# Full attention with every engine's order written out, small jobs in a queue, and row sums through a column of ones

## The chip, the cores and the metric

The kernel runs on one core of one Trainium2 chip. The metric is the device time of one execution in microseconds (us). Engine names are those of the profile: PE (TensorE matmuls), PEld (its weight loads), DVE (VectorE), ACT (ScalarE), POOL (GpSimd), SP (SyncE, which issues most DMAs).

## The reference

Input x has 1024 tokens (a grid of 16 rows by 64 columns) of width 1024. Cut to what matters:

```
h = rmsnorm(x)                                  # gain_in
p = h @ w                                       # 1024 x 3328: q,k,v of A; q,k,v of B; gates of A and of B
A: 8 query heads, 2 key/value heads, D = 64; q, k RMS-normalised per head, 2-D axial rotary positions;
   softmax(q k^T / 8) v over all 1024 keys
B: 8 heads, D = 64; each token sees 8 grid rows x 16 columns around it;
   softmax(q k^T / 8 + relative bias, masked) v
y = concat(A * silu(gate_a), B * silu(gate_b)) @ w_out
out = rmsnorm(x + y)                            # gain_out
```

Everything is float32 in and out.

## The kernel before

Weights come in 17 groups of 256 columns, g = 0 to 12 of w and 13 to 16 of w_out. A product in near float32 accuracy is three fp16 matmuls: the activations and the weights are each split into hi (fp16 of the scaled value) and lo (fp16 of the rest), and hi·hi, hi·lo and lo·hi go to one PSUM tile. So a weight group is loaded by POOL's queue (L158), squared by ACT for its scale (L280), summed over partitions by a tiny matmul (L292) whose result DVE and POOL turn into the scale (L293, L294), split into hi by ACT (L299, two halves) and lo by DVE (L306, two halves); PE then uses it (L368). Two raw tiles rotate: group g + 2 is loaded once g is split.

Four stages follow one another. The **head** loads and normalises x, transposes it and projects the groups that A needs. **A** has 64 units, each a head and a block of 128 queries. A unit does QK into a PSUM tile of 128x1024 (L591, L593), the row maximum on DVE (L600, called MAX below), the exponential on ACT in fp32 (L602) with the row sum in its accumulator, its fp16 hi on ACT (L603), its lo on DVE (L608, LO), one DMA transpose of hi and lo on SP (L613) and, four units later, 24 matmuls with V's hi and lo (L622 to L624, pv). After every fourth unit DVE divides by the row sums (L628 to L631). **B** has 64 units, each a head and a block of 128 queries with two or three key blocks (256 or 384 keys): QK (L674, L675), biased maximum on DVE (L682, L684), two exponentials on ACT (L685 with its accumulator, L686), LO on DVE (L691), transpose, pv five units later (L704 to L706), division and gate (L711 to L716). The biases are built ahead by DVE from a loaded table and a mask (L648), one instruction of 128x1536 for each of four tables. The **tail** has the output rows that are left: row u of eight needs its mixture squared, scaled and split (L732 to L744, called os(u)), transposed (L749), and 24 matmuls for each of four groups, added to the residual (L773) and normalised (L797 to L807).

One object, `Flow`, keeps the order. Each unit is a slot (`step`): "pre" callbacks, QK and MAX, "mid" callbacks, LO of the unit before, "post" callbacks, then `fill(n)`, which takes n pieces of six projection matmuls from a queue, then pv of an older unit. `at(delay, pos, fn)` puts a callback into a later slot. FILL_A and FILL_B give n by slot. PE's order is always that of the code; in A and B, before, the order of ACT, DVE, POOL and SP is the scheduler's, which may put a ready instruction ahead of an earlier one. SPLIT_AT says after which unit of B os(u) starts.

Of the kernel before, what the change touches and what calls it, by code (L numbers as in the profile page):

```python
# [8 lines left out]
F32 = mybir.dt.float32  # L9
# [13 lines left out]
NX = 4  # L23
SKEW_A, SKEW_B = 4, 5
# [5 lines left out]
PREP = {2: 4, 3: 0, 4: 2, 12: 0, 13: 0}  # L30
# [3 lines left out]
AREA = 34816  # L34
RING = 5
SLOTS = {"both": (16384, 2048, 4), "qc": (24576, 2048, 2), "stg1": (28672, 2048, 3), "stg": (18432, 2048, 3),
         "t": (0, 1536, 5), "ptb": (7680, 1536, 5), "ob": (15360, 1024, 1), "th": (16384, 16384, 2), "y": (16384, 2048, 1),
         "p32": (AREA + 14336, 1536, 2)}
BIAS = {(0, 0): ("ar", 18432), (0, 1): ("rq", 8192), (1, 0): 0, (1, 1): 1}
# [4 lines left out]
class Flow:  # L44


    def __init__(self):
        self.slot = 0
        self.due = {}
        self.queue = []  # L50
        self.credit = 0.0

    def at(self, delay, pos, fn, *a):
        self.due.setdefault((self.slot + delay, pos), []).append((fn, a))

# [18 lines left out]
    def step(self, n, first=None, second=None, last=None):  # L74
        self.run("pre")
        if first:
            first()
        self.run("mid")
        if second:
            second()  # L80
        self.run("post")
        self.fill(n)
        if last:
            last()
        self.run("end")
        self.slot += 1
# [3 lines left out]
def kernel(ctx: ExitStack, tc: tile.TileContext, x: bass.AP, w: bass.AP, wo: bass.AP,  # L90
# [14 lines left out]
    at = fl.at  # L105
# [8 lines left out]
    ar = one.tile([P, 25, 512], F32, name="ar").rearrange("p a b -> p (a b)")  # L114
# [39 lines left out]
    def load_w(g):  # L154
# [3 lines left out]
        pool.dma_start(raw[g], w[g] if g < 13 else wo[g - 13])  # L158

# [73 lines left out]
    def x_sq(u, e):  # L233
        xhl[u] = one.tile([P, 2, 1024], F16, tag=f"m{u % 4}", name=f"xhl{u}")
# [35 lines left out]
    def prep_a(g):  # L270
# [7 lines left out]
        wss[g] = tn(f"wss{g}", 1, "ws")  # L278
        if g:
            act.activation(wp[g][0].bitcast(BF16), raw[g], AF.Square, accum_out=wss[g])  # L280
            return
        late["half"] = tn("wssh", 1, "ws")
        act.activation(wp[g][0][:, :4].bitcast(BF16), raw[g][:, :4], AF.Square, accum_out=late["half"])

    def prep_a2(g):
        dve.tensor_tensor_reduce(out=wp[g][0][:, 4:].bitcast(BF16), in0=raw[g][:, 4:], in1=raw[g][:, 4:], scale=1.0,
                                 scalar=late["half"], op0=OP.mult, op1=OP.add, accum_out=wss[g])

    def prep_b(g):
        pt = ahead.append(proj_tile(f"wt{g}")) or ahead[-1]  # L290
        top = [a.bitcast(BF16)[:, 1:2] for a in (mh[:, :1], wss[g])]
        pe.matmul(pt[:, 0, :1], top[0].to_broadcast([P, P]), top[1], start=True, stop=True)  # L292
        dve.tensor_scalar(wss[g], pt[:, 0, :1], -2.0 ** -27, 1e-30, op0=OP.mult, op1=OP.add)  # L293
        pool.tensor_tensor(col(S_ + g), wss[g], mh[:, :1], op=OP.pow)  # L294
# [6 lines left out]
    def prep_d(g):  # L301
# [7 lines left out]
        if g > 14:  # L309
            t = wraw.tile([P, 2, 1024], F32, tag="raw", name=f"x2{g}")  # L310
            for i in range(2):
                x2[2 * g - 26 + i] = t[:, i]
                load_x2(2 * g - 26 + i)

    ready = set()
# [18 lines left out]

    def prep(g):
        d = PREP.get(g, 1)
        at(d + 1, "pre", prep_a, g)
        at(d + 2, "mid", pend.append, g)

    def sums_now():  # L340

        while pend:
            g = pend.pop(0)
            prep_b(g)
            at(1, "pre", prep_c, g)
            at(1, "post", prep_d, g)
            if g + 2 < 17:
# [27 lines left out]
    def proj_pair(g, up, lhs, evac):  # L375

        pt = proj_tile(f"pj{g}_{up}")
        assert g in ready
# [15 lines left out]
    va = r6(1, [P, NU, 2, 2, D], F16, "va")  # L394
# [57 lines left out]
    def kva_gen(up):  # L452
        def evac(pt):
# [3 lines left out]
            at(1, "pre", lambda: act.activation(va[:, 2 * up:2 * up + 2, :, 0, :], vs, AF.Copy, scale=2.0 ** -14))  # L457

            def vlo():
                for i in range(2):  # L460
                    dve.scalar_tensor_tensor(va[:, 2 * up + i, :, 1, :], vs[:, i], 2.0 ** -14,
                                             va[:, 2 * up + i, :, 0, :], op0=OP.mult, op1=OP.subtract)
# [26 lines left out]
    def qb_gen(hh, up):  # L489
        def evac(pt):  # L490
# [15 lines left out]
            at(1, "pre", hi)  # L506
            at(1, "mid", lo)
# [536 lines left out]
```

## Time and profile before

| what | value |
|---|---|
| median of 3 runs | 604.59 us (600.97 to 606.09) |
| the profiled execution's own time | 600.28 us |
| its span | 598.5 us |
| mean granted TensorE clock | 0.974 |
| busy in the span: PE, DVE, ACT, POOL | 530.8, 440.9, 391.0, 121.8 us |
| stages on the span: head, A, B, tail | 0 to 105, to 352, to 557, to 598.5 us |

A window row of the profile reads: its bounds, its length, then for PE, PEld, DVE, ACT and POOL the busy time and the count of instructions in brackets, then the granted clock (1.00 is full), the mean busy share of the 16 DMA engines and GB/s. A wait row reads: engine, operation and line that waited, what released it, then total us, times and the longest. A group row reads: line, engine, operation, out<-in, shapes, count, then busy us and mean ns of one, then idle time ahead of it and its releasers. A timeline row reads: start, duration, engine, line, operation, and in brackets idle time ahead of it.

### The profile page before, as it was taken

The numbers are of one execution on the slowest core, as the hardware profiler recorded it, in microseconds if no ns is written. First come the engines' busy times: TensorE is split into PE (matmuls) and PEld (weight loads), VectorE is DVE, ScalarE is ACT, GpSimd is POOL, SyncE is SP. The second block draws the span as 40 slices with busy tenths as digits, with TensorE's granted clock in tenths as the row PEclk, the third lists the DMA queues.
The fourth block names the chain that finished last, engine by engine and source line by source line (L and its number), as shares of the span: only waits on it lengthen the run. The fifth ranks groups of instructions, "written<-read, shape, count | busy, mean of one in ns | idle before, by whom it ended". The sixth has DMA issues, their size and how long they took to land.

```text
span 598.5 us, 13870 instructions
## 1 busy us (share of the span) xinstructions
PE 530.8 (89%) x5541; PEld 404.4 (68%) x5541; DVE 440.9 (74%) x986; ACT 391.0 (65%) x647; POOL 121.8 (20%) x150
## 2 busy tenths in 40 slices
PE   2587989979979989998989979999999789889894
PEld 1366878758856545556768857887877567668684
DVE  4689676987978968975988947585878767778332
ACT  5553445777768858875868826677779986774210
POOL 2395788510100000000100000010111221122100
PEclk9979989989999989999899999999999899999898
DMA  8989533799999999999899983467576996699422
GB/s 233 225 162 243 112 108 68 143 187 215 195 192 188 206 209 181 221 191 208 179 188 213 230 214 79 90 133 96 128 116 123 180 200 146 138 146 190 92 61 70
DMA packets 245972, 97.26 MB, mean 162 GB/s; under 512 B 236562, under 2 KB 237202, under 8 KB 243987
## 3 DMA queue, kind: packets, MB, share of 16 engines
q1 hardware_dynamic: 242306, 75.66, 70.8%
q0 software_dynamic: 3312, 19.92, 11.7%
q8 instruction: 43, 0.70, 0.5%
q10 hardware_dynamic: 288, 0.79, 0.5%
q14 instruction: 23, 0.18, 0.1%
HBM read 31.33 MB, written 4.19 MB: 59 GB/s over the span
## 4 chain that ended last, share of the span: by engine, by line
PE 48%; DMA 18%; DVE 14%; issue 8%; ACT 5%; POOL 4%; SPq 1%; DVEq 0%; POOLq 0%; ACTq 0%
PE pj L368 15%; DMA ar<-ar 10%; PE wt L368 8%; PE kb L368 5%; PE po L368 4%; PE s L591 3%; PE s L593 3%; PE pv L622 2%; PE pv L624 2%; PE pv L623 2%; DVE whl L306 2%; DMA ar<-mhl 2%; POOL nt L416 1%; PE sb L675 1%; DMA x2b<-in_x_dram 1%
## 5 line engine op out<-in xcount | busy, mean ns | idle before, releaser
L368 PEld LDWEIGHTS <-hT 128*128 128x128 f16 x2112 | 205.8, 100 | 68.9 <-DMA hT<-xhl 14.7
L368 PE MATMUL pj<-whl,hT 128*128 128x256 f16 x1584 | 187.6, 274 | 3.9 <-DMA hT<-xhl 2.5
L602 ACT ACTIVATE ar<-s,nm,sm 128x1024 f32<-128x1024 f32 x64 | 76.9, 1202 | 43.6 <-DVE nm L600 35.8
L600 DVE CUSTOM_DVE_ANT_0 ar<-s,sm 128x1024 bf16<-128x1024 f32 x64 | 81.9, 1279 | 18.9 <-PE s L593 18.6
L368 PE MATMUL wt<-whl,hT 128*128 128x256 f16 x528 | 70.9, 294 | 13.8 <-ACT whl L299 7.1
L608 DVE TENSOR_TENSOR ar<-ar 128x1024 f16<-128x1024 f32 x64 | 77.9, 1218 | 5.4 <-ACT ar L603 5.4
L603 ACT ACTIVATE ar<-ar 128x1024 f16<-128x1024 f32 x64 | 67.5, 1056 | 6.5 <-DVE ar L608 5.3
L368 PE MATMUL po<-whl,mA 128*128 128x256 f16 x384 | 65.8, 277 | 0.0
L685 ACT ACTIVATE rq<-ar,mx,sm 128x384 f32<-128x384 f32 (+1 forms) x64 | 43.0, 672 | 30.8 <-DVE mx L684 30.6
L294 POOL TENSOR_TENSOR sm<-wss,mh 128x1 f32<-128x1 f32 x17 | 12.7, 749 | 240.4 <-DVE wss L293 160.6
L368 PEld LDWEIGHTS <-mA 128*128 128x128 f16 x512 | 48.8, 100 | 12.5 <-issue 5.3
L368 PE MATMUL po<-whl,ar 128*128 128x256 f16 x192 | 53.1, 277 | 0.0
L622 PE MATMUL pv<-va,ar 128*128 128x64 f16 x384 | 39.9, 195 | 12.0 <-DMA ar<-ar 12.0
L306 DVE SCALAR_TENSOR_TENSOR whl<-raw,sm,whl 128x1024 f16<-128x1024 f32 (+1 forms) x33 | 44.7, 1371 | 2.3 <-ACT whl L299 2.3
L622 PEld LDWEIGHTS <-ar 128*128 128x128 f16 x384 | 35.1, 99 | 16.6 <-DMA ar<-ar 14.3
L686 ACT ACTIVATE ar<-ar,mx,sm 128x384 f16<-128x384 f32 (+1 forms) x64 | 42.8, 673 | 1.0
L299 ACT ACTIVATE whl<-raw,sm 128x1024 f16<-128x1024 f32 x34 | 37.0, 1136 | 5.9 <-POOL sm L294 5.8
L624 PE MATMUL pv<-va,ar 128*128 128x64 f16 x384 | 39.9, 195 | 0.0
L623 PE MATMUL pv<-va,ar 128*128 128x64 f16 x384 | 39.8, 195 | 0.0
L591 PE MATMUL s<-kTa,rq 128*128 128x512 f16 x128 | 39.4, 391 | 0.3 <-ACT ar L602 0.3
L682 DVE CUSTOM_DVE_ANT_0 ar<-sb,bias 128x384 f32<-128x384 f32 x48 | 26.6, 554 | 17.2 <-PE sb L675 14.3
L691 DVE TENSOR_TENSOR ar<-rq,ar 128x384 f16<-128x384 f32 (+1 forms) x64 | 34.1, 533 | 4.4 <-ACT ar L686 4.4
(183 smaller groups left out, 1012.2 us busy)
## 6 DMA issues: line engine op xcount, KB each, us to landing
raw<-in_w_dram POOLq DMA_DIRECT2D x11, 1024.0 KB, 6.3
raw<-in_wo_dram POOLq DMA_DIRECT2D x4, 1024.0 KB, 6.1
ar<-in_x_dram SPq DMA_DIRECT2D x7, 512.0 KB, 6.4
khh<-ar SPq DMA_DIRECT2D x16, 128.0 KB, 4.1
x2b<-in_x_dram POOLq DMA_DIRECT2D x4, 512.0 KB, 6.4
x<-in_x_dram POOLq DMA_DIRECT2D x4, 512.0 KB, 6.3
out_dram<-x2b SPq DMA_DIRECT2D x8, 256.0 KB, 3.3
ar<-ar SPq DMA_TRANSPOSE x112, 4.5
```

Of the source, the lines that this page charges most:

```text
L306: dve.scalar_tensor_tensor(wp[g][1][:, s], raw[g][:, s], col(S_ + g), wp[g][0][:, s], op0=OP.mult, op1=OP.subtract)
L368: pe.matmul(*o[0], **o[1])
L591: pe.matmul(s[:, c * 512:(c + 1) * 512], q, kTa[:, 4 * c:4 * c + 4, hh], start=True, stop=False)
L600: dve.tensor_tensor_reduce(out=hl[:, 1].bitcast(BF16), in0=s, in1=col(SHA).to_broadcast([P, 1024]), scale=col(NSA), scalar=3e38, op0=OP.ad ...
L602: act.activation(p32, s, AF.Exp, bias=nm, scale=col(SCA), accum_out=sums[hh, u][:, h:h + 1])
L603: at(0, "post", lambda: act.activation(hl[:, 0], p32, AF.Copy))
L608: dve.tensor_tensor(hl[:, 1], p32, hl[:, 0], op=OP.subtract)
L622: pe.matmul(o, pt[:, kt], va[:, kt, hh, 0], start=kt == 0, stop=False)
L623: pe.matmul(o, pt[:, kt], va[:, kt, hh, 1], start=False, stop=False)
L624: pe.matmul(o, pt[:, 8 + kt], va[:, kt, hh, 0], start=False, stop=kt == 7)
L685: act.activation(p32, t, AF.Exp, bias=mx, scale=col(SCB + hh), accum_out=sums["b", u][:, h:h + 1])
L686: act.activation(hl[:, 0], t, AF.Exp, bias=mx, scale=col(SCB + hh))
```

## The change

Every line number of the changed kernel is about 110 to 115 higher in A and B (MAX is L713, EXP L715, HI L716, LO L721, pv L735 to L737, hi and lo of the weights L386 and L391, bias L761, B's MAX L796).

- **A by hand.** From the sixth slot of A to its end ACT, DVE, POOL and SP also follow the order of the code. In B the scheduler orders them as before.
- **Jobs with a budget.** Small work of ACT and DVE goes into a list (`job`) with a cost in us and a lateness. In each slot `work(eng)` takes the jobs due, urgent ones always, others while half their cost fits into what a slot's budget leaves (BASE_A or BASE_B plus 0.654 us per piece of filler, less the engine's fixed work). `need` forces the jobs of a weight group or an output row out before PE's first use.
- **Weights.** From group 5 squares are taken in four quarters into spare space as soon as the load is there, their sums by four tiny matmuls, hi and lo in quarters; the next load follows one slot after the last lo.
- **Column of ones.** V has 65 columns, the last one 1.0, so pv with hi of V also yields the row sum; the exponentials no longer write an accumulator, and the division reads PSUM.
- **Gates of A** do two steps on POOL and one on DVE, instead of two on DVE. **os(u)** squares one half on ACT and the other on DVE, and its steps are jobs.
- **Biases** are built by one job per head; the masks of the three tables made in B go into a tile that A's last transposed p used ("gain"), and gain_out is loaded into it at slot 16 of B.
- **Order of output work.** Rows 4, 5 and 6 are in B's queue (before, row 4 only), with other FILL_B and SPLIT_AT.

```diff
-FILL_B = [(12, 3.4), (24, 3), (2, 2.5)]
-FILL_B_END = 3
-SPLIT_AT = (26, 27, 29, 31, 39, 55, 56)
+FILL_B = [(13, 3.25), (12, 2.95), (22, 3.45)]
+FILL_B_END = 3.2
+SPLIT_AT = (22, 24, 27, 31, 39, 47, 55)
...
+    def work(self, eng):
+
+        b = self.budget.get(eng)
+        self.left[eng] = 1e9 if b is None else min(self.left.get(eng, 0.0), 0.5 * b) + b
+        while True:
+            due = sorted(j for j in self.jobs if j[3] == eng and j[1] <= self.slot and (j[0] == 0 or j[4] / 2 < self.left[eng]))
+            if not due:
+                return
+            j = due[0]
+            self.jobs.remove(j)
+            self.left[eng] -= j[4]
+            j[5](*j[6])
...
+        if self.base:
+            us = self.base[0] + 0.654 * n
+            self.budget = {"act": us - self.base[1], "dve": us - self.base[2]}
         self.run("pre")
+        self.work("act")
         if first:
             first()
-        self.run("mid")
         if second:
             second()
+        self.run("mid")
+        self.work("dve")
         self.run("post")
...
+        def lo(i):
+            q = QUARTERS[i]
+            dve.scalar_tensor_tensor(wp[g][1][:, q], raw[g][:, q], col(S_ + g), wp[g][0][:, q], op0=OP.mult, op1=OP.subtract)
+            if i < 3:
+                return
+            ready.add(g)
+            prep_e(g)
+            if g + 2 < 17:
+                at(1, "pre", load_w, g + 2)
...
-        act.activation(p32, s, AF.Exp, bias=nm, scale=col(SCA), accum_out=sums[hh, u][:, h:h + 1])
-        at(0, "post", lambda: act.activation(hl[:, 0], p32, AF.Copy))
+        act.activation(p32, s, AF.Exp, bias=nm, scale=col(SCA))
+        at(0, "mid", lambda: act.activation(hl[:, 0], p32, AF.Copy))
...
-            pe.matmul(o, pt[:, kt], va[:, kt, hh, 0], start=kt == 0, stop=False)
-            pe.matmul(o, pt[:, kt], va[:, kt, hh, 1], start=False, stop=False)
-            pe.matmul(o, pt[:, 8 + kt], va[:, kt, hh, 0], start=False, stop=kt == 7)
+            pe.matmul(o, pt[:, kt], va[:, kt, hh, v_hi], start=kt == 0, stop=False)
+            pe.matmul(o[:, :D], pt[:, kt], va[:, kt, hh, v_lo], start=False, stop=False)
+            pe.matmul(o, pt[:, 8 + kt], va[:, kt, hh, v_hi], start=False, stop=kt == 7)
...
-    run_units(ua, SKEW_A, a_qk, a_lo, a_pv, rates(FILL_A + [(64 - n_head, mid)], FILL_A_END))
-    fl.fill(1000)
-
-    gout = one.tile([P, 1024], F32, tag="gain", name="gain_o")
-    sp.dma_start(gout, dap(gain_out, 0, [[0, P], [1, 1024]]))
+    fl.base = BASE_A
+    with run_units(ua, SKEW_A, a_qk, a_lo, a_pv, rates(FILL_A + [(64 - n_head, mid)], FILL_A_END), by_hand=HAND):
+        fl.fill(1000)
+
...
+    ms = one.tile([P, 1024], F32, tag="gain", name="masks")
...
+                make = load_bias(ty, hh, ms[:, ty * 384:ty * 384 + 384], k < 2)
+                for h in range(4):
+                    job("dve", 0.5, make, h, delay=2 + 2 * k, late=1)
```

The first place is DVE in the second row block of A, where a weight group is split into lo. In the names nm is a unit's row maximum, s its scores, ar its exponentials, whl the split weights, raw the loaded ones. Before:

```order
L600 ISA ar,nm_6_1_2429<-s_6_1_2424,sm 128x1024
L600 ISA nm_6_1_2429 128x1
L318 RECIPROCAL sm<-sm 128x1
L608 TENSOR_TENSOR ar<-ar 128x1024
L320 TENSOR_SCALAR sm<-sm 128x1
L306 SCALAR_TENSOR_TENSOR whl_2277<-raw_1368,sm,whl_2277 128x1024
L353 TENSOR_TENSOR sm<-sm 128x1
L306 SCALAR_TENSOR_TENSOR whl_2277<-raw_1368,sm,whl_2277 128x1024
L600 ISA ar,nm_6_2_2487<-s_6_2_2482,sm 128x1024
```

And after, for the same weight group:

```order
L721 TENSOR_TENSOR ar<-ar 128x1024
L391 SCALAR_TENSOR_TENSOR whl_2224<-raw_1365,sm,whl_2224 128x512
L713 ISA ar,nm_5_3_2364<-s_5_3_2359,sm 128x1024
L713 ISA nm_5_3_2364 128x1
L721 TENSOR_TENSOR ar<-ar 128x1024
L644 SCALAR_TENSOR_TENSOR klo<-kb_0_0_2226,ar 128x512
L713 ISA ar,nm_6_0_2409<-s_6_0_2404,sm 128x1024
```

Two halves in one slot have become quarters that stand behind LO in several slots.

The second place is DVE where A ends and B begins: mx is the maximum of a unit of B, bias_… and rq and ar the bias tables, masks their masks, pv_7 the last sums of A. Before:

```order
L608 TENSOR_TENSOR ar<-ar 128x1024
L648 SCALAR_TENSOR_TENSOR bias_4648<-bias_4648,sm,ar 128x1536
L551 SCALAR_TENSOR_TENSOR ar<-wt_4233,ar 128x4x64 x2
L361 TENSOR_TENSOR vf_4769<-sm 128x1
L648 SCALAR_TENSOR_TENSOR rq<-rq,sm,ar 128x1536
L362 TENSOR_SCALAR sm<-vf_4769 128x4
L551 SCALAR_TENSOR_TENSOR ar<-pj_3_4485,ar 128x4x64 x2
L631 TENSOR_TENSOR mA_1065<-pv_7_4457,sum_7_4208 128x256
L682 ISA ar,mx_0_4619<-sb_4612,ar 128x256
L682 ISA mx_0_4619 128x1
L684 TENSOR_SCALAR mx_0_4619<-mx_0_4619,sm 128x1
L682 ISA ar,mx_1_4654<-sb_4612,ar 128x256
```

After:

```order
L796 ISA ar,mx_0_4701<-sb_4695,ar 128x256
L796 ISA mx_0_4701 128x1
L391 SCALAR_TENSOR_TENSOR whl_4712<-raw_3762,sm,whl_4712 128x512
L742 TENSOR_SCALAR sum_7_4708<-sum_7_4708,sm 128x4
L391 SCALAR_TENSOR_TENSOR whl_4712<-raw_3762,sm,whl_4712 128x512
L798 TENSOR_SCALAR mx_0_4701<-mx_0_4701,sm 128x1
L761 SCALAR_TENSOR_TENSOR rq<-rq,sm,masks 128x384 x4
L391 SCALAR_TENSOR_TENSOR whl_4712<-raw_3762,sm,whl_4712 128x512
L744 TENSOR_TENSOR ar<-pv_7_4528,sum_7_4708 128x256
L761 SCALAR_TENSOR_TENSOR bias_4732<-bias_4732,sm,masks 128x384 x3
L796 ISA ar,mx_1_4741<-sb_4695,ar 128x256
```

Two bias tables that stood ahead of the first maximum of B now stand between the first and the second one, and weight quarters stand among them.

More of the change, by code (lines that the diff above doesn't have):

```diff
@@ L594, in a_qk @@
                       start=False, stop=True)
-        if h == 0:
-            sums[hh, u] = tn(f"sum{hh}_{u}", 4, "sum")
         nm = tn(f"nm{hh}_{u}_{h}")
@@ L717, in evac @@
                 ready.add(("b", u, hh))
-            at(1, "mid", evac)
+            job("dve", 0.85, evac, late=0)
     mT, rws, osp = {}, {}, {}
@@ L774, in then @@
         def then():
-            at(1, "mid", add)
+            job("dve", 0.5 * len(jobs), add, late=0)
             if jobs[-1] == (1, 13):
```

314 lines of the change are left out of this document (205 added, 109 removed).

## The prediction

> **What bounds the kernel now.** I read the page's first part, then the windows by stage, then PE's waits inside each stage, then the rows of the steps that the change touches. The first part gives the ranking:
>
> ```profile
> PE 530.8 (89%) x5541; PEld 404.4 (68%) x5541; DVE 440.9 (74%) x986; ACT 391.0 (65%) x647; POOL 121.8 (20%) x150
> ```
>
> PE is busy for 89% and no other engine comes near over the whole. The profiled execution took 600.28 us, 1.8 more than its span; my sum goes against that. It is 4.3 below the median of 604.59, so the forecast is the sum plus 4.3.
>
> The stages, cut at the program's seams (head; full attention, A; neighbourhood attention, B; tail), with busy time and count for PE, PEld, DVE, ACT and POOL, then granted clock, DMA share and GB/s:
>
> ```profile
> 0.00:105.00 105.00, 80.10 (x613) 63.65 (x614) 73.17 (x139) 52.65 (x83) 69.38 (x77) 0.95 0.72 165
> 105.00:352.00 247.00, 228.17 (x2707) 162.02 (x2705) 203.92 (x342) 182.85 (x250) 18.49 (x19) 0.98 1.08 197
> 352.00:557.00 205.00, 189.05 (x1929) 149.62 (x1929) 149.14 (x468) 149.04 (x301) 30.50 (x48) 0.99 0.71 140
> 557.00:598.50 41.50, 33.45 (x294) 29.14 (x294) 14.68 (x38) 6.46 (x17) 3.42 (x6) 0.92 0.26 64
> 124.00:128.00 4.00, 4.00 (x25) 2.35 (x22) 3.04 (x6) 2.82 (x3) 1.12 (x1) 0.58 1.27 143
> 216.00:220.00 4.00, 3.66 (x31) 2.19 (x32) 0.45 (x1) 0.83 (x1) 0.00 (x0) 0.57 1.19 238
> 284.00:288.00 4.00, 3.91 (x35) 2.65 (x36) 4.00 (x10) 2.41 (x4) 0.00 (x0) 0.57 0.62 136
> 476.00:480.00 4.00, 4.00 (x29) 2.76 (x28) 1.62 (x5) 3.67 (x8) 0.14 (x1) 0.63 1.02 283
> 304.00:308.00 4.00, 4.00 (x52) 3.17 (x51) 3.41 (x6) 2.85 (x5) 0.00 (x0) 1.00 1.03 194
> ```
>
> A has 247.0 − 228.2 = 18.8 us of PE idleness, B 16.0, the tail 8.1. In A the DVE is busy for 83%: A is bound by PE with DVE close behind. Four windows show a clock of 0.57 to 0.63; such a stretch costs about 4 × (1 − 0.57) = 1.7 us. The waits of PE in A, then in B (total, times, longest):
>
> ```profile
> PE pv L622 <- DMA ar<-ar: 12.0, 6, 2.7
> PE wt L292 <- DVE ar L501: 3.6, 1, 3.6
> PE wt L292 <- DVE rq L551: 2.5, 1, 2.5
> ```
>
> ```profile
> PE wt L368 <- DVE whl L306: 6.9, 5, 2.9
> PE sb L674 <- DVE mx L682: 2.4, 2, 1.8
> PE wt L368 <- ACT whl L299: 2.4, 2, 2.1
> PE sb L704 <- DMA ar<-ar: 1.9, 2, 1.0
> ```
>
> In A the price is six transposes of p that come late and two evacuations of projections. In B it is weights that are split into hi and lo only as PE reaches them (6.9 + 2.4 = 9.3). The transposes are late in this way (the weight load on POOL; SP's transposes, two that took 8.39 us; and PE's first matmul after them, with the gap ahead of it in brackets):
>
> ```profile
> 204.58 0.57 POOL L158 DMA_DIRECT2D raw<-in_w_dram  x1 [5.11 <-DVE whl L306]
> ```
>
> ```profile
> 207.61 8.39 SPq L613 DMA_TRANSPOSE ar<-ar  x2
> ```
>
> ```profile
> 216.34 0.23 PE L622 MATMUL pv<-va,ar 128*128 128x64 f16 x1 [2.51 <-DMA ar<-ar]
> ```
>
> A split of two lo halves occupies DVE, LO of a unit goes out late, the raw load for the group after next starts the moment the split is done, and two transposes share the DMA engines with it.
>
> **The change part by part.** The rows that price it:
>
> ```profile
> L600 DVE CUSTOM_DVE_ANT_0 ar<-s,sm 128x1024 bf16<-128x1024 f32 x64 | 81.9, 1279 | 18.9 <-PE s L593 18.6
> L608 DVE TENSOR_TENSOR ar<-ar 128x1024 f16<-128x1024 f32 x64 | 77.9, 1218 | 5.4 <-ACT ar L603 5.4
> L306 DVE SCALAR_TENSOR_TENSOR whl<-raw,sm,whl 128x1024 f16<-128x1024 f32 x32 | 42.4, 1341 | 2.3 <-ACT whl L299 2.3
> L570 DVE SCALAR_TENSOR_TENSOR mA<-ar,sm,mA 128x512 f32<-128x512 f32 x8 | 6.0, 747 | 0.0
> L744 DVE SCALAR_TENSOR_TENSOR mhl<-mA,os,mhl 128x512 f16<-128x512 f32 x8 | 6.0, 748 | 0.3 <-ACT mhl L740 0.3
> L648 DVE SCALAR_TENSOR_TENSOR rq<-rq,sm,ar 128x1536 f32<-128x1536 f32 x1 | 1.8, 1819 | 6.1 <-DMA ar<-in_colmask_dram 6.1
> ```
>
> ```profile
> L602 ACT ACTIVATION_READ_ACCUMULATOR ar<-s,nm,sm 128x1 f32 x64 | 12.3, 193 | 0.0
> L685 ACT ACTIVATION_READ_ACCUMULATOR rq<-ar,mx,sm 128x1 f32 x64 | 12.0, 187 | 0.0
> ```
>
> *Order of A.* A split is now four quarters of 128x512, spread over several slots behind that slot's MAX and LO; the nearest row for a quarter is L744's 748 ns. MAX plus LO of a unit are 1279 + 1218 = 2.50 us of DVE, and 2.5 plus one quarter is 3.25, just inside what PE needs: 228.2 / 68 slots = 3.36 (now 247 / 68 = 3.63). Four quarters cost 2.99 against two halves' 2.68, so DVE's total in A stays near 204, that is 3.0 a slot. No burst of 2.68 us stands ahead of a LO any more, so the transposes leave evenly. Bounds for the 12.0 of pv waits: 0, and 12.0 if the load alone causes them. I take 3 left, because the load, still issued in A, is now one slot past the last quarter. The single waits of 3.6 and 2.5: the first falls when the hand order is only beginning, and I leave 3 of it; the second goes. Slow stretches in A: three now, one or two after, −2.5. What is late next in A is DVE itself, 3.0 of work in 3.4 of slot. A: −9 − 0.6 − 2.5 − 2.5 = −14.6.
>
> *Weights of B.* Their splits are queued to end before PE's first use in three groups of four, and in the same slot in the fourth; 9.3 becomes 1.5, and the bounds are 0 and 9.3. The squares move from L280 into four small ACT pieces earlier, hidden by ACT's 25% idleness in B (149 of 205); without cover they would be +1 a group. B: −7.8. Whether the slow stretch at 476 goes is open; I let it stay.
>
> *Entry of B.* The three bias tables are made in twelve jobs of 128x384 instead of three of 1819 ns, among the first MAXs on a DVE that runs in order. Their masks now use the tile that the last pv of A reads, so their DMA starts only after that. Behind a waiting bias job on DVE stand a weight quarter, the evacuation and MAX b1; for MAX b1 waits PE's third QK, and for that PE's filler. The entry costs 2.4 on PE now while one bias waits 6.1 for its mask, a wait that the scheduler's order put where nobody was behind it. Bounds: 0 and 2.4 + 6.1 = 8.5; I take 4.5, nearer 2.4, because PE holds projections between the QKs. Add 0.9 for half a chance of a slow stretch. Entry: +3.0.
>
> *Column of ones.* The two rows of accumulator reads, 24.3 us of ACT, go; ACT was 74% busy in A and ended only one short wait of PE, so they are worth 0 on the path (a gain is bounded by the 2.4 that ACT ended in B). The price is on PE: 64 × 16 + 352 = 1376 pv matmuls are one column wider. The spacing of pv matmuls and of projection matmuls:
>
> ```profile
> 234.74 0.19 PE L622 MATMUL pv<-va,ar 128*128 128x64 f16 x1
> ...
> 235.41 0.19 PE L624 MATMUL pv<-va,ar 128*128 128x64 f16 x1
> ```
>
> ```profile
> 357.66 2.14 PE L368 MATMUL pj<-whl,hT 128*128 128x256 f16 x18
> ...
> 359.63 0.27 PE L674 MATMUL sb<-khh,qTb 128*128 128x256 f16 x1
> ```
>
> The first are 24 matmuls, so (235.41 − 234.74) / 23 = 29 ns; the second are 18 in 1.97 us, 109 ns each. That is (109 − 29) / 192 = 0.42 ns a column, 0.6 us for 1376. No row shows 65 columns; the upper bound is a second 29 ns for each, 40 us. I take 0.6, plus 0.5 for 36 more tiny matmuls of the weight sums: +1.1.
>
> *Gates and small things.* The second gate step of A's groups (L570, 8 × 747 ns) leaves DVE for POOL, which has 175 us free in B, and no wait of PE hangs on it: 0.
>
> *Tail.* 96 matmuls of output rows (10.5 us at 109 ns) move from behind the last pv into B, where they are work all the same; in their place after the last pv stand 96 instead of 192 as cover for row 7's preparation. That chain now (evacuation; transposes of mhl, the last):
>
> ```profile
> 557.47 0.42 DVE L714 TENSOR_TENSOR ar<-sb,sumb 128x256 f32<-128x256 f32 x1 [1.15 <-PE sb L706]
> ```
>
> ```profile
> 568.27 1.23 SPq L749 DMA_TRANSPOSE ar<-mhl  x1
> ```
>
> It lasts from 557.5 to 569.5, 12.0 us. In it DVE stands ahead of its lo halves in an add that waits for matmuls:
>
> ```profile
> 564.38 0.88 DVE L773 SCALAR_TENSOR_TENSOR x<-po,rw,x 128x256 f32<-128x256 f32 x2 [2.23 <-PE po L368]
> ```
>
> Without that wait of 2.23 it is 10, so 10 to 12 against 10.5 is a stall of 0 to 1.5; with another such add in the chain and a late transpose (2.2 and some 3) a miss of 5 could come. I take +1.5.
>
> *Sum.* 600.28 − 14.6 − 7.8 + 3.0 + 1.1 + 1.5 = 583.5 in the profiled frame; 587.8 by the median.
>
> **A rule beside the rows.** Two gaps of PE, the first ahead of the slow window at 124, the second ahead of the window 304 to 308:
>
> ```profile
> 123.21 0.16 PE L292 MATMUL wt<-wss,mh 128*128 128x1 bf16 x1 [3.58 <-DVE ar L501]
> ...
> 302.55 0.20 PE L622 MATMUL pv<-va,ar 128*128 128x64 f16 x1 [2.69 <-DMA ar<-ar]
> ```
>
> The slow windows of A follow gaps of 3.58, 2.51 (216.34) and 2.5 (the wait on L551), yet the gap of 2.69 is followed by a clock of 1.00. The Trainium skill, "TensorE: Matmul & The Clock Gate", Part 1, "HAM oscillation", says that the clock halves after an idle stretch above about 3.4 us. The trace agrees for the gap of 3.58, and not for the two others, where 2.5 were enough. By that rule shorter gaps would change nothing of two of A's three slow stretches, and the third gap mostly stays, so none of the 2.5 is gained: the sum would be 586.0 in the profiled frame instead of 583.5.
>
> **The rivals.**
>
> *The DMA sets A's pace (chance 0.15).* In A the DMA share is 1.08 and its rate 197 GB/s; the bytes and the transposes stay the same. If late transposes come from that traffic and not from DVE's bursts, the pv waits and their slow stretches stay, about 9 + 1.7 of the gain is lost: 598.5. For it: two transposes in 8.39 us just after a load. Against: only some six of 64 are late.
>
> *DVE in a fixed order becomes A's bound (slower, chance 0.13).* By hand the engine cannot run a ready instruction past a waiting one. MAX and LO are 2.5, the jobs come to 0.5 to 1.2 a slot, and each slot has a handover to wait for: the scheduler's DVE idled 18.6 for S and 5.4 for HI. If the average slot is over 3.63 A gets longer. At 2.5 + 0.8 + (18.6 + 5.4) / 68 = 3.65 it begins; with 1.0 of jobs it is 3.85, A +15 instead of −14.6: 587.8 + 29.6 = 617. Against: 204 us of DVE work fit in 232 if the waits overlap PE's own need.
>
> *65 columns cost twice (0.02).* 587.8 + 39 = 627: slower.
>
> *The seams eat it (0.12).* Entry at 8.5 + 1.7, cover missed by 5, weights in B late by half (4.6): 587.8 + 4.8 + 3.5 + 3.1 = 599, within 1%.
>
> **How the numbers follow.** The forecast, 587.8, has 0.58; its own spread is ±8 from the pv waits (3 to 9), the entry (0 to 8.5) and the tail. The range runs from 573 (all waits of A and B's weights at 0, entry at 0: 587.8 − 3 − 3 − 1.5 − 5.4 − 1.5) to 606, which takes in the DMA's rival and the seams and leaves out the two slower ones, 0.15, and a little below. One per cent, about what a measurement of this kernel can tell, is 598.5 to 610.6. Faster: 0.58 + half of the DMA's rival and of the seams, 0.13 = 0.71; same: the other half, 0.14, and 0.02 for a DVE that is only a little late, 0.16; slower: 0.13, the rest of the two slower rivals.
>
> **What would show it.** Right, if in A PE's waits on transposes fall to about 3 us, A takes some 232 us with DVE near 88%, and in B no wait of PE on the weights' lo is over 1.5. The entry is right if PE waits 3 to 6 us on the first MAXs, the tail if PE idles under 2 us before row 7. The forecast is wrong if PE's waits in A are now for MAX or S (DVE bound), if pv spacing is over 35 ns, or if transposes still land in 8 us beside a load and pv waits for them.

## The result and the profile after

The changed kernel takes 595.84 us (median of four runs, 593.98 to 597.55), the kernel before beside it 603.1: a ratio of 0.990, 95% interval 0.986 to 0.994. That is 6 to 7 us faster where 15 to 17 were forecast. Here and below a time is the median of all runs of a kernel, and a ratio leaves out runs that took over 1.5% longer than the fastest of the same kernel. The profiled execution of the changed kernel took 597.55 us, the slowest of its four, and that of before 600.28, less than any of the four beside it, so the two traces lie only 2.7 us apart.

The first part of the page after:

```profile
PE 531.3 (89%) x5577; PEld 406.4 (68%) x5577; DVE 453.7 (76%) x1022; ACT 387.9 (65%) x599; POOL 139.3 (23%) x175
```

PE is as busy as before, to 0.5 us. The windows, cut at the same seams (head, A, B, tail), then three of the four stretches of A with a slow clock, with the columns of the prediction:

```profile
0.00:105.00 105.00, 76.84 (x608) 62.16 (x609) 73.17 (x138) 51.99 (x82) 69.50 (x78) 0.95 0.72 163
105.00:355.50 250.50, 232.99 (x2731) 165.06 (x2729) 207.13 (x356) 186.69 (x235) 15.58 (x29) 0.97 1.06 192
355.50:565.50 210.00, 200.21 (x2050) 160.81 (x2051) 161.13 (x497) 143.65 (x270) 51.37 (x64) 0.99 0.70 141
565.50:595.80 30.30, 21.27 (x192) 18.36 (x190) 12.24 (x33) 5.57 (x14) 2.90 (x5) 0.93 0.31 70
224.00:228.00 4.00, 4.00 (x35) 1.97 (x34) 2.43 (x3) 2.74 (x4) 0.00 (x0) 0.68 1.11 208
296.00:300.00 4.00, 3.13 (x38) 2.13 (x39) 0.97 (x4) 1.31 (x2) 0.68 (x3) 0.78 1.05 254
320.00:324.00 4.00, 3.30 (x39) 2.13 (x40) 1.77 (x7) 2.14 (x3) 0.75 (x5) 0.77 1.26 165
```

A is no shorter. Cut more sharply, at the first QK of each stage and the last QK of B, the two profiled executions compare as follows (before, after, difference in us):

| stretch | before | after | difference |
|---|---|---|---|
| start to A's first QK | 101.43 | 102.00 | +0.6 |
| A: to B's first QK | 251.5 | 255.1 | +3.6 |
| B: to its last QK | 189.4 | 193.6 | +4.2, with 10.5 us of output rows more |
| from there to the end | 56.2 | 45.1 | −11.1, with these 10.5 us less |

"A" below is always that second stretch. In this pair of traces the gain lies wholly behind A, where B and the end together are 6.9 us shorter. PE's waits in A after (total, times, longest):

```profile
PE pv L735 <- DMA ar<-ar: 5.6, 4, 2.0
PE wt L360 <- DVE ar L614: 5.2, 2, 2.8
PE wt L360 <- DVE rq L665: 3.8, 2, 1.9
PE pv L735 <- DMA pt<-ar: 2.0, 2, 1.5
PE s L706 <- ACT ar L715: 1.6, 1, 1.6
```

The pv waits have gone from 12.3 to 7.6, but the tiny matmuls of the weight sums (wt L360) now wait 9.0 for DVE to evacuate a projection, where two waits of 3.6 and 2.5 stood. How such a wait arises is seen on DVE, and then on PE:

```profile
293.72 1.28 DVE L713 CUSTOM_DVE_ANT_0 ar<-s,sm 128x1024 bf16<-128x1024 f32 x1
...
294.93 1.22 DVE L721 TENSOR_TENSOR ar<-ar 128x1024 f16<-128x1024 f32 x1
296.06 0.75 DVE L665 SCALAR_TENSOR_TENSOR rq<-pj,rq 128x256 f16<-128x256 f32 x2
```

```profile
296.87 0.25 PE L360 MATMUL wt<-wss,mh 128*128 128x1 bf16 x4 [1.88 <-DVE rq L665]
```

The evacuation L665 stands behind MAX and LO of its slot. The sum, which comes in the middle of a projection pair, asks for the PSUM tile that this evacuation frees, and PE stands still behind it. And the transposes still meet a load. Its issue on POOL, the transpose beside it on SP, and PE's matmul that waits for one:

```profile
212.38 0.57 POOL L204 DMA_DIRECT2D raw<-in_w_dram  x1 [20.15 <-ACT ar L716]
```

```profile
214.38 5.34 SPq L726 DMA_TRANSPOSE ar<-ar  x1
```

```profile
221.94 0.20 PE L735 MATMUL pv<-va,ar 128*128 128x65 f16 x1 [1.97 <-DMA ar<-ar]
```

In B the waits on weights are gone, and waits for MAX have come:

```profile
PE sb L789 <- DVE mx L796: 5.6, 7, 2.1
PE sb L818 <- DVE mx L796: 3.0, 2, 1.8
PE wt L477 <- DVE whl L391: 0.3, 1, 0.3
```

The largest of them, on DVE (weight quarters and an output add ahead of a MAX, the next MAX 2.3 us behind) and then on PE (the QK that starts as the second of these ends):

```profile
503.29 0.87 DVE L904 SCALAR_TENSOR_TENSOR x2b<-po,rw,x2b 128x256 f32<-128x256 f32 x2
...
504.15 1.40 DVE L391 SCALAR_TENSOR_TENSOR whl<-raw,sm,whl 128x512 f16<-128x512 f32 x2
505.46 0.55 DVE L796 CUSTOM_DVE_ANT_0 ar<-sb,bias 128x384 f32<-128x384 f32 x1
...
507.73 0.56 DVE L796 CUSTOM_DVE_ANT_0 ar<-sb,bias 128x384 f32<-128x384 f32 x1
```

```profile
508.34 0.32 PE L789 MATMUL sb<-khh,qTb 128*128 128x384 f16 x1 [2.14 <-DVE mx L796]
```

### The profile page after: what moved, and what is told of

It is laid out like the page before. It is cut to its first block, busy times and chain, and to the rows that moved or that the text cites. A ratio compares the mean times of both kernels' runs of the same rounds, so it can differ in the third digit from the quotient of the medians.

```text
span 595.8 us, 13972 instructions
## 1 busy us (share of the span) xinstructions
PE 531.3 (89%) x5577; PEld 406.4 (68%) x5577; DVE 453.7 (76%) x1022; ACT 387.9 (65%) x599; POOL 139.3 (23%) x175
## 4 chain that ended last, share of the span: by engine, by line
PE 53%; DVE 18%; DMA 13%; issue 8%; POOL 4%; ACT 3%; SPq 1%; DVEq 0%; POOLq 0%; ACTq 0%
PE pj L477 13%; PE wt L477 10%; PE kb L477 5%; DMA ar<-ar 5%; PE po L477 5%; PE s L708 4%; PE s L706 4%; PE pv L735 2%; PE pv L736 2%; PE pv L737 2%; DMA pt<-ar 2%; DVE whl L391 2%; DVE ar L713 1%; PE sb L790 1%; DVE mhl L871 1%
## 5 line engine op out<-in xcount | busy, mean ns | idle before, releaser
L477 PE MATMUL pj<-whl,hT 128*128 128x256 f16 x1488 | 176.9, 274 | 4.8 <-DMA hT<-ar 3.1
L715 ACT ACTIVATE ar<-s,nm,sm 128x1024 f32<-128x1024 f32 x64 | 76.9, 1202 | 47.7 <-DVE nm L713 38.1
L713 DVE CUSTOM_DVE_ANT_0 ar<-s,sm 128x1024 bf16<-128x1024 f32 x64 | 82.0, 1281 | 31.1 <-PE s L708 30.5
L477 PE MATMUL wt<-whl,hT 128*128 128x256 f16 x624 | 79.9, 284 | 15.8 <-DVE ar L303 6.6
L477 PEld LDWEIGHTS <-ar 128*128 128x128 f16 x768 | 73.2, 99 | 14.3 <-issue 4.0
L721 DVE TENSOR_TENSOR ar<-ar 128x1024 f16<-128x1024 f32 x64 | 78.7, 1230 | 2.9 <-ACT ar L716 2.9
L477 PE MATMUL po<-whl,ar 128*128 128x256 f16 x672 | 80.1, 276 | 1.0 <-DMA ar<-mhl 1.0
L716 ACT ACTIVATE ar<-ar 128x1024 f16<-128x1024 f32 x64 | 67.7, 1058 | 3.2 <-DVE wss L362 0.8
L735 PE MATMUL pv<-va,ar 128*128 128x65 f16 x384 | 40.6, 194 | 5.6 <-DMA ar<-ar 5.6
L735 PEld LDWEIGHTS <-ar 128*128 128x128 f16 x384 | 35.8, 97 | 9.6 <-DMA ar<-ar 7.4
L363 POOL TENSOR_TENSOR sm<-wss,mh 128x1 f32<-128x1 f32 x17 | 9.8, 577 | 136.8 <-DVE wss L362 136.0
L736 PE MATMUL pv<-va,ar 128*128 128x64 f16 x384 | 40.6, 195 | 0.0
L737 PE MATMUL pv<-va,ar 128*128 128x65 f16 x384 | 40.5, 193 | 0.0
L796 DVE CUSTOM_DVE_ANT_0 ar<-sb,bias 128x384 f32<-128x384 f32 x48 | 26.5, 553 | 15.4 <-PE sb L790 8.8
L204 POOL DMA_DIRECT2D raw<-in_w_dram x11 | 6.6, 602 | 131.5 <-ACT ar L716 81.1
L736 PEld LDWEIGHTS <-ar 128*128 128x128 f16 x384 | 35.7, 98 | 2.2
L391 DVE SCALAR_TENSOR_TENSOR whl<-raw,sm,whl 128x512 f16<-128x512 f32 x48 | 37.0, 795 | 0.2 <-ACT whl L386 0.2
```

What stands on the lines that cost most here:

```text
L391: dve.scalar_tensor_tensor(wp[g][1][:, q], raw[g][:, q], col(S_ + g), wp[g][0][:, q], op0=OP.mult, op1=OP.subtract)
L477: pe.matmul(*o[0], **o[1])
L713: dve.tensor_tensor_reduce(out=hl[:, 1].bitcast(BF16), in0=s, in1=col(SHA).to_broadcast([P, 1024]), scale=col(NSA), scalar=3e38, op0=OP.ad ...
L715: act.activation(p32, s, AF.Exp, bias=nm, scale=col(SCA))
L716: at(0, "mid", lambda: act.activation(hl[:, 0], p32, AF.Copy))
L721: dve.tensor_tensor(hl[:, 1], p32, hl[:, 0], op=OP.subtract)
```

## The experiments

The first question is A. My theory was that its gain went into the sums' waits; the rivals were that DVE in a fixed order sets A's pace, and that weight loads keep the transposes late whatever DVE does. The runs with "before" in their name start from the kernel before, all others from the changed kernel. Ratios are to the kernel before on the same chip.

### The changed kernel again

> The changed kernel as it is, on the chip of the next three, so that they have it beside them. Every theory: a ratio to before of 0.985 to 0.994, and in full attention PE's waits of the weight sums on projection evacuations (DVE's lo) near 9 us, on transposes near 7 us.

0.989 (0.985 to 0.994); ten runs lie between 589.85 and 602.44. In its trace A took 254.6 us, with pv waits of 6.4 and sums' waits of 9.0. One and the same program thus varies by 2% from run to run, and one comparison of medians with few runs can be half a per cent off. The clock goes with it: the mean granted clock was 0.984 in the fastest of the ten and 0.962 in the slowest, and 0.022 of 600 us is 13 us, about as much as the two lie apart. An estimate of each run without its slow clock, its time less (1 − clock) × its span, lies between 579.0 and 581.0 us for nine of the ten.

A run further below (B by hand), whose edit touches B alone, gives another execution of the same A. The rows of A, here and there:

```profile
101.74:356.31 254.57, 238.08 (x2780) 169.70 (x2777) 208.29 (x359) 189.72 (x238) 17.47 (x31) 0.97 1.03 191
```

```profile
103.88:351.79 247.91, 231.53 (x2780) 166.22 (x2777) 207.93 (x355) 189.20 (x237) 18.38 (x31) 0.99 1.05 193
```

PE does the same work and idles 16.5 and 16.4 us, with the same waits on sums, 9.0, and pv waits of 6.4 and 6.2. The difference of 6.7 us is PE's busy time at a slower clock. So A's length in one execution, the +3.6 above included, says little by itself, and the tests below are read by PE's waits first.

### Sums two pieces later

```diff
-            yield from chunks(ops, 6, (lambda: evac(pt)) if i else None)
+            if 3 <= g <= 8:
+                yield from chunks(ops, 6, (lambda: evac(pt)) if i else (lambda: None), 12 if i else 0)
+            else:
+                yield from chunks(ops, 6, (lambda: evac(pt)) if i else None)
...
+            elif i + n == sums_at:
+                sums_now()
```

> One edit on the changed kernel: in groups 3 to 8 the tiny matmuls of a weight sum come two pieces (12 matmuls) later in a projection pair, so that the PSUM tile that they take has been evacuated. Theory (the gain of full attention went into waits of the weight sums on evacuations, 9.0 us in four waits, and the slow-clock stretches behind three of them, 3 x 1.7): those waits fall under 1.5 us and the time is 8 to 14 us below the changed kernel, 582 to 588. Rival (DVE in its fixed order sets full attention's pace): the waits only change their name, to MAX or transposes, and the time is less than 3 us below.

590.12 us, 0.977 (0.970 to 0.984). PE's waits in A:

```profile
PE pv L740 <- DMA ar<-ar: 6.9, 5, 1.9
PE pv L740 <- DMA pt<-ar: 3.0, 3, 2.3
PE wt L360 <- DVE ar L619: 2.6, 1, 2.6
```

The sums' waits fell from 9.0 to 2.6 and A from 254.6 to 248.2, under the 8 expected at least; pv waits rose from 6.4 to 9.9. So I ran it again, with more rounds:

> The run with sums later once more, with more rounds: if its gain over the changed kernel is real, the ratio to before stays at 0.970 to 0.983, below the changed kernel's interval of 0.985 to 0.994.

595.74 us, 0.988 (0.983 to 0.993): the gain did not hold. The sums' waits are 2.6 again, but pv waits were 18.7 and A took 256.8 us, and one load makes most of the difference. Its issue, then PE's first pv behind it, in this execution and then in the first:

```profile
158.82 0.57 POOL L204 DMA_DIRECT2D raw<-in_w_dram  x1 [22.50 <-ACT ar L720]
```

```profile
171.93 0.24 PE L740 MATMUL pv<-va,pt 128*128 128x65 f16 x1 [8.60 <-DMA pt<-ar]
```

```profile
162.07 0.57 POOL L204 DMA_DIRECT2D raw<-in_w_dram  x1 [24.18 <-ACT ar L721]
```

```profile
172.15 0.20 PE L740 MATMUL pv<-va,ar 128*128 128x65 f16 x1 [1.91 <-DMA ar<-ar]
```

The same program waits 1.9 us behind a load in one execution and 8.6 in another.

### Loads cut to an eighth

```diff
+        if 5 <= g <= 10:
+            raw[g] = raw[g - 2]
+            pool.dma_start(raw[g][:, :1], w[g][:, :1])
+            squares(g, 4)
+            return
```

> The changed kernel, with the loads of weight groups 5 to 10 cut to an eighth (128 KB instead of 1 MB; the rest of the tile keeps the group before, so the results are not the reference's). Theory (the transposes that are late in full attention are those that share the DMA engines with a weight load): PE's waits of pv on transposes in full attention fall from 6 to 8 us to under 1.5, while the waits of sums on evacuations stay at 9. Rival (they are late because DVE issues LO late): pv waits stay over 5.

590.32 us in one run, a time that the changed kernel itself reaches (589.85); A took 246.9 us. Its waits:

```profile
PE wt L365 <- DVE ar L619: 5.5, 2, 2.8
PE wt L365 <- DVE rq L670: 3.8, 2, 1.9
PE pv L740 <- DMA ar<-ar: 1.0, 1, 1.0
```

pv waits fall to 1.4 (0.4 of them on another tile) and the sums' stay: the late transposes are the loads' doing. Even the 1.4 comes behind a load, the only whole one in A behind the cut ones, that of group 11:

```profile
343.00 0.58 POOL L209 DMA_DIRECT2D raw<-in_w_dram  x1 [28.18 <-issue]
```

```profile
345.08 0.20 PE L740 MATMUL pv<-va,ar 128*128 128x65 f16 x1 [0.97 <-DMA ar<-ar]
```

The same cut in the kernel before:

> The kernel before, with the loads of weight groups 5 to 10 cut to an eighth in the same way. It tells whether the 12.0 us of pv waits before came from the loads too, or, as the prediction had it, from bursts of weight splits on DVE ahead of LO. By the loads: pv waits under 2. By the bursts: over 8. A mix lies between.

590.3 us in one run; pv waits fall from 12.3 to 3.9 and A from 251.5 to 241.0. Of the 3.9, 2.5 come behind the load of group 11, whole here too (issued at 326.54 us), and 1.4 do not. So before the change, too, nearly all of the waits came behind loads, though the bursts on DVE were still there.

### Sums later in the kernel before

> The kernel before, with the weight sums of groups 3 to 8 two pieces later in a pair. If a sum that asks for its PSUM tile too early costs the kernel before, too, its waits of 6.1 us fall under 2 and two slow-clock stretches go: 594 to 598, a ratio near 0.99. If the scheduler's order had hidden it, nothing changes.

606.46 us, 1.011 (1.004 to 1.017): slower, which nobody expected. The sums' wait fell from 6.1 to 0.7, and its place was taken:

```profile
PE pv L627 <- DMA ar<-ar: 14.3, 9, 4.2
PE pv L627 <- DMA pt<-ar: 2.8, 1, 2.8
```

pv waits rose from 12.3 to 17.1 and A stayed at 252.1. A pause of PE at a sum seems to be time in which the transposes catch up; that is a reading, which the runs with both edits test.

### Both at once, and the loads doubled

> The changed kernel with both edits: loads of groups 5 to 10 cut to an eighth (the results are not the reference's) and the weight sums of groups 3 to 8 two pieces later. If each wait is its own loss, full attention loses both: 248 - 7 or so, 236 to 240 us from its first QK to the first QK of neighbourhood attention, with under 5 us of waits. If the transposes alone already set the stage's pace, it stays at 245 or more and pv waits come back.

576.27 us in one run, and A took 235.7 us. The waits:

```profile
PE wt L365 <- ACT ar L725: 2.6, 1, 2.6
PE pv L745 <- DMA ar<-ar: 1.6, 1, 1.6
PE pv L745 <- DMA pt<-ar: 1.6, 1, 1.6
```

The cut loads alone took 7.7 off A, the later sums alone between 6.4 and nothing, both 18.9. PE's idle time in A fell from 16.5 to 11.2 with the cut loads, to 15.0 with later sums (first execution) and to 6.6 with both: 5.3, 1.5 and 9.9, so the two waits hide each other in part. The other 9.0 of the 18.9 is PE's busy time, 238.1 in the changed kernel and 229.1 with both, where the granted clock in A is 1.00: no slow stretch is left. It is one execution of each. That the transposes catch up while PE waits is borne out in part: with the loads cut, too, later sums raise pv waits, from 1.4 to 3.2 here, and from 3.9 to 7.1 in the kernel before (next run). DVE is no bound here, nor are the transposes by themselves.

> The kernel before with both edits, loads of groups 5 to 10 cut to an eighth and sums two pieces later. It gives full attention's length without loads and sums' waits in the scheduler's order; by PE's busy time it would be 232 to 236 us. If the changed kernel's is shorter with the same two edits, the order by hand is better where nothing else limits it; if longer by 2 to 3, that is the 65th column.

590.34 us in one run, A 239.2, above the 232 to 236 expected, with pv waits of 7.1 left although the loads are cut (3.4 of them behind the whole load of group 11). So with loads and sums out of the way the changed kernel's A is 3.5 us shorter than that of before, and the whole 14: 576 against 590. The opposite test:

> The changed kernel with the loads of weight groups 5 to 10 issued twice, into the same tile (the work is the same). If bytes loaded beside the transposes set their delay, pv waits in full attention go from 7 to 14 us or more and the stage grows by 7 or more. If a load delays transposes only by its start, they stay under 9.

612.23 us in one run, A 270.5, 15.9 longer:

```profile
PE pv L736 <- DMA pt<-ar: 9.1, 4, 3.6
PE pv L736 <- DMA ar<-ar: 7.7, 4, 4.4
```

pv waits go from 6.4 to 16.8. Six megabytes more cost 16 us of A: 11.5 of idle time and 4.5 of busy time, at a clock of 0.95 against 0.97.

### Three other ways to issue the loads

```diff
+            for i in range(4):
+                q = slice(2 * i, 2 * i + 2)
+                if i:
+                    at(i, "pre", lambda q=q: pool.dma_start(raw[g][:, q], w[g][:, q]))
+                else:
+                    pool.dma_start(raw[g][:, q], w[g][:, q])
```

> The changed kernel with sums later as in the run before, the sums of groups 3 and 4 one piece later still, and the loads of weight groups 5 to 10 issued in four quarters of 256 KB, one per slot. If loads delay the transposes by their length, four short collisions fit into the 4 to 5 us that a transpose has to spare: pv waits fall from 10 to under 4, sums' waits to 0, and the time is 5 to 9 us below the run with sums later alone, near 583. If it is the sum of bytes that counts, the waits spread over more slots and the time stays at 590.

600.13 us, 0.988 (0.982 to 0.994), and no test of what was meant: nothing holds POOL, so for four of the six groups it issued all four quarters within 1.7 us. In the profiled execution pv waits came to 21.2, with one of 6.2 behind four such quarters. Then with a hold, a copy that reads the row maximum of the slot before:

```diff
+                    if "nm" in late:
+                        pool.tensor_copy(raw[g][:, 2 * i, :1], late["nm"])
+                    pool.dma_start(raw[g][:, q], w[g][:, q])
```

> Like the run with loads in quarters, but each quarter's load on POOL stands behind a copy of one column that reads the row maximum of the slot before, so that the quarters really go out one a slot (without that POOL issued two to three of them within 1.6 us). Theory (a load delays the transposes by what is in flight beside them; a quarter is inside the slack of one transpose): pv waits in full attention under 4 us (10 with whole loads, 20 with four quarters at once), and 583 to 588. Rival (transposes alone fill the DMA engines, DMA share 1.0, so every byte loaded delays them): pv waits stay at 7 or more and the time at 590 or above.

599.83 us, 0.990 (0.984 to 0.996). The quarters went out 1.7 to 6.2 us apart, pv waits were 9.5, with the longest, 3.5, after a group's last quarter: pacing does not remove them, though beside 9.9 and 18.7 with whole loads one trace can't say whether it eases them. Sums' waits were 4.5, and PE waited 2.6 more for DVE to read a sum. Last, eighths on SP, each behind a transpose:

```diff
+            for k in range(KC):
+                at(k, "post", lambda k=k: sp.dma_start(raw[g][:, k], w[g][:, k]))
```

> Sums later, and the loads of groups 5 to 10 issued by SP in eighths of 128 KB, one behind each transpose, so that they stand in line with the transposes instead of running beside them from POOL's queue. If a transpose is delayed because a whole load is in flight beside it, pv waits in full attention fall under 5 us (10 to 15 with whole loads) and the time is 580 to 588. If the DMA engines have no room for the bytes in any order, pv waits stay at 8 or more and the time at 592 or above.

604.61 us, 1.001 (0.997 to 1.005); A 262.4, pv waits 18.8. SP's own queue shows the cost. The first row is an eighth of a load, the second a transpose of p:

```profile
154.21 0.61 SPq L206 DMA_DIRECT2D raw<-in_w_dram  x1
154.92 3.10 SPq L736 DMA_TRANSPOSE ar<-ar  x1
```

A transpose of p occupies SP's queue for 1.5 to 5.8 us, 2.7 in the median, of a slot that here lasts 3.9 (262.4 / 68), and a transpose of q, in eight of the slots, for 1.25 more. All that SP issues in A occupies it for 234.5 of the 262.4 us, against 208.4 of 255.1 in the changed kernel's first trace; that this is what makes the transposes later is my reading, not shown.

### The order in A, undone and shifted

> One edit on the changed kernel: in full attention ACT, DVE, POOL and SP are ordered by the scheduler again; jobs, quarters, ones column and the rest stay. Theory (the order by hand wins 4 us of transpose waits and loses 3 us of evacuation waits): within 4 us of the changed kernel; sums' waits near 6, transposes' near 12. Rival (the order by hand is what the change gains by): 7 us slower than the changed kernel or more, as slow as before. Second rival (the order by hand costs, the rest of the change gains): 5 us faster or more.

593.87 us, 0.988 (0.982 to 0.994): as fast as the changed kernel. A took 253.3, pv waits 12.9, sums' waits 2.5. The scheduler's order leaves A where it was, with the waits exchanged.

> One edit on the changed kernel: in full attention the urgent jobs of DVE (evacuations among them) stand ahead of LO instead of behind it, as the callbacks before the change did. Theory (the sums wait because the hand order puts evacuations behind LO, 1.22 us): the four waits shrink by about 1.2 us each, from 9.0 to 4 to 5 us, and transposes wait a little more. Rival (the position of the sum alone counts): they stay above 8.

594.3 us in one run; sums' waits 5.7, pv waits 11.8, A 251.0. The place of evacuations behind LO makes over a third of the sums' waits, a little less than expected, and the transposes take more than that back: PE's waits in A are 19.0, against 16.4. A is shorter all the same, at a granted clock of 0.99 against 0.97.

### The column of ones

> One edit on the changed kernel: pv is 64 columns wide again and the row sums come from the accumulators of the exponentials again (128 reads of 0.19 us on ACT, 24 us). Theory (ACT's reads lie beside PE's work, the 65th column costs PE 1.5 ns for each of 1376 matmuls): 2 us faster than the changed kernel, between 0 and 4. Rival (ACT's relief is on the path): 3 us slower or more.

601.67 us, 0.995 (0.991 to 0.999), beside 0.989 (0.985 to 0.994) with the column: if anything slower without it. And on top of the later sums:

> Sums later, but with pv of 64 columns and the row sums from the exponentials' accumulators. The first comparison had the kernel without the ones column 3.5 us slower, with intervals that touch. If the ones column pays (ACT's 24 us of reads are on somebody's path), this is 2 to 6 us slower than sums later beside it; if it only costs PE its 2 us, it is 1 to 3 us faster.

597.49 us, 0.989 (0.983 to 0.995), beside 0.988. Neither the expected 2 us of gain nor a sure loss: in neither pair is the kernel with the column the slower one, and in neither is the difference clear of noise. A group of 24 pv matmuls took 0.70 us before, 0.73 with the column, and 0.72 in this kernel, whose V has the new layout and 64 columns: the column itself costs 0.01 a group, 0.6 us over A, and the layout of V 0.02, 1.3. Without the column PE's waits for MAX in B were 9.0 and 12.9 us, beside 8.3 and 6.3 with it on the same chips, but also 9.0 with it in the first run with later sums; whether ACT's reads delay DVE there is not shown.

### B by hand

```diff
-    with run_units(ub, SKEW_B, b_qk, b_lo, b_pv, rates(FILL_B, FILL_B_END), hooks2, by_hand=1000):
+    with run_units(ub, SKEW_B, b_qk, b_lo, b_pv, rates(FILL_B, FILL_B_END), hooks2, by_hand=0):
```

> One edit on the changed kernel: neighbourhood attention, too, follows the order of the code on ACT, DVE, POOL and SP. PE's waits on its MAX there are 8.6 us in the changed kernel. Theory (the scheduler puts weight quarters and output adds ahead of MAX, and the order of the code would not): the MAX waits fall under 4, the stage shortens by 3 us or more. Rival (DVE is short of time there in any order, or the masks' DMA then stands ahead of a MAX): the stage is as long or longer.

600.29 us in one run; B took 201.8 us against 195.3. The waits for MAX are gone, and these came:

```profile
PE po L477 <- DVE whl L391: 6.5, 1, 6.5
PE wt L477 <- DMA ar<-mhl: 5.3, 2, 4.6
```

In this one run the scheduler's putting weight quarters ahead of MAX is the cheaper of the two.

## Why the prediction was wrong

The sign was right and the range held the time, but the forecast was more than twice the gain, and the step that failed is **the order of A**, −14.6 us where the trace has +3.6. The rest of the sum misses by 4 the other way.

**pv waits, 12.0 to 3: wrong in its cause.** I said that a burst of weight splits on DVE makes LO late, and that spreading it lets transposes leave evenly. The cut loads show that the load beside them is the cause (12.3 to 3.9 before, 6.4 to 1.4 after, and 2.5 and 1.4 of what is left stand behind the load that was not cut). The row that I quoted, two transposes of 8.39 us just behind a load, said so, and I gave that rival 0.15 because only some six of 64 transposes are late. But A before has seven loads, and PE's matmuls behind those six waits start 9 to 17.5 us after the issue of a load: two after that of 160.17, one each after those of 204.58, 248.13, 293.85 and 336.58. The change moved the load by a slot; 7.6 us stayed in the first trace.

**The waits on evacuations, 6.1 to 3: became 9.0.** I priced the two waits as accidents of the old order and did not follow the new order of the evacuation itself, which moved from ahead of LO to behind it. Moving it back takes 3.3 off (9.0 to 5.7), moving the sum takes 6.4 off.

**Slow stretches, −2.5: +1.7.** There are four in A instead of three; each window's missing clock times 4 us adds up to some 1.7 a stretch. Two follow sums' waits of 1.88 us. The Trainium skill, "TensorE: Matmul & The Clock Gate", "HAM oscillation", would have needed 3.4; this trace has slow windows behind gaps of 1.88 and 1.97, while the longest gap in A is followed by full clock. The gap, and the window behind it:

```profile
138.75 0.24 PE L360 MATMUL wt<-wss,mh 128*128 128x1 bf16 x4 [2.75 <-DVE ar L614]
```

```profile
140.00:144.00 4.00, 4.00 (x58) 3.31 (x57) 2.04 (x3) 0.71 (x1) 0.00 (x0) 1.00 1.20 170
```

In the trace of the changed kernel again a gap of 2.75 at the same sum (138.00) is followed by a slow stretch, as are its two gaps of 1.88; in the run with B by hand gaps of 2.76 and twice 1.88 at the same places are not. The length of a single gap does not decide here, and a forecast of A's slow stretches from its gaps could only be luck: there are five of them in the one execution of this A and one in the other.

**The column of ones, +0.6 and nothing on ACT: the column's price about right, the layout left out.** The column was 0.6 over A (0.4 was A's share of the estimate); the layout of V around it adds 1.3, which I had not counted. From the first of 24 pv matmuls to the last it is now 0.71 us (237.15 to 237.86), 31 ns each. That ACT's relief is worth nothing is not refuted: the runs without the column leave it open.

So A, in this pair of traces: pv waits −4.7, evacuations +2.5 (with 0.5 on a projection that went), QK behind ACT in the first slots +1.4, slow stretches +1.7, pv matmuls +2.0, in all +2.9 of the 3.6.

**Weights of B, −7.8: right.** 9.3 became 0.3. **Entry, +3.0: too dear.** PE waits 1.98 there, 1.77 before. What I did not see is where the waits would turn up: the same quarters, with two more rows' steps on DVE, stand ahead of MAX late in B, and of the 8.6 us of MAX waits 5.1 fall between 481 and 509 us. B as a whole is 6.3 shorter when the moved 10.5 are taken off, against 4.4 by my terms. **Tail, +1.5: −0.6.** PE waits 1.0 on row 7's transposes.

**The rivals.** That DMA sets A's pace (0.15) is the one that came, in its mechanism: late transposes come from the loads, and most of the pv waits and the slow stretches stayed. That its time, 598.5, is near the measured 595.8 is partly luck: pv waits did fall by 4.7, and sums, pv matmuls and the rest of the sum, which it does not name, moved both ways. DVE in a fixed order did not become the bound: with the loads cut and the sums later, the same order runs A in 235.7 us, as short as my forecast for it (251.5 − 14.6 = 236.9 in this stretch).

What stays open is why the wait behind one load is 1.9 us in one execution and 8.6 in another, what decides whether a slow stretch follows a gap, and whether the version with later sums is faster than the changed kernel at all: 0.977 and 0.988 against 0.989 and 0.990. No version here is surely better than the changed one.

## What to carry to other kernels

Line the late transfers up in time with the transfers that could make them late: here each of six waits stood behind a load, which was reason enough to test that cause before forecasting. Before pricing a wait as gone, cut its supposed cause in a run that leaves the work out, together with the next wait in line, since two waits of which each gives the other time to catch up may show little when only one is removed. Split a stage's length into idle time and busy time before comparing two executions: the same matmuls took 231.5 and 238.1 us here. When an order is written by hand, follow each small step that frees a buffer, and ask who takes that buffer next, and when.

## What the runs showed of the hardware

A load of 1 MB that POOL issues stretches the transposes that SP issues beside it. In the first run with later sums, two transposes on SP's queue, the first issued just ahead of the load of 162.07, and the times of all 48 on that tile (ns, shortest, median, longest):

```profile
161.51 11.16 SPq L731 DMA_TRANSPOSE ar<-ar  x2
```

```profile
L731 SPq DMA_TRANSPOSE ar<-ar x48: 1471/2512/7179, 114.9 to 338.9; - x48
```

The first occupies the queue for 7.2 us, the second, issued as the load lands, for 3.9, where 2.5 is the median; the one beside the load of 212.38 above took 5.3. Not every one beside a load is long, and a few with no load in flight take nearly 5 us. The Trainium skill, "DMA: Bandwidth & Descriptors", "Queues, rings and completion order", says that each DMA engine takes turns between its queues a packet at a time; the trace agrees in that the transposes go on, slower, and no run here shows the turns themselves. An eighth of a load issued on SP held that queue for 0.6 us.

Four loads of 256 KB were no gentler than one of 1 MB in these traces: pv waits of 21.2 at once and 9.5 paced, beside 9.9 and 18.7 with whole loads. And one program, on one chip, took between 589.85 and 602.44 us in ten runs, at mean granted clocks from 0.984 to 0.962, with the same gaps of PE followed by a slow stretch in one execution and by full clock in another.
